# A hybrid decoder block on one core: block sums of the tokens with four operations a round, and a third raw tile for the memory's weights

## The chip, the cores and the metric

The kernel runs on one core of a Trainium2 chip. The metric is the device time of one execution in microseconds; the times of before are those of three runs. TensorE (PE, with its weight loads PEld), VectorE (DVE), ScalarE (ACT), GpSimd (POOL) and the DMA queue of SyncE (SP) each work through their own list of instructions in order, and wait for each other by semaphores.

## The reference

One decoder layer over 1024 tokens of width 1024, all in float32. Three gated branches read the same normalised tokens; what is computed, cut to what matters here:

```python
h = rmsnorm(x, g_mix_norm[l])
proj = jnp.einsum('bsd,de->bse', h, w_in[l])
sb_q, sb_k, sb_v, fx_q, fx_k, fx_v, f_logit, m_q, gate_logit = split_columns(proj, SPLITS)
o_sb = stick_breaking_attention(...)      # 8 heads of 64
o_fox = forgetting_attention(...)         # 8 heads of 64
mh = rmsnorm(mem, g_mem_norm[l])          # 256 memory tokens
mkv = jnp.einsum('bmd,de->bme', mh, w_mem_kv[l])
mk, mv = split_columns(mkv, (D_MEM, D_MEM))
mq, mk = rmsnorm(...), rmsnorm(...)
o_mem = memory_attention(mq, mk, mv)      # 4 heads of 128
merged = gates[:, :, 0] * br_sb + gates[:, :, 1] * br_fox + gates[:, :, 2] * br_mem
x = x + jnp.einsum('bsd,de->bse', merged, w_out[l])
u = jax.nn.relu(jnp.einsum('bsd,df->bsf', rmsnorm(x, g_mlp_norm[l]), w_ff_up[l]))
x = x + jnp.einsum('bsf,fd->bsd', u * u, w_ff_down[l])
```

## The kernel before

**Products.** Each float32 operand is split into a high part, rounded by ScalarE, and a low part, which VectorE makes by a subtraction. A product is three matmuls: high by high, high by low, low by high. A weight therefore goes through a fetch into a raw tile, ScalarE (`split`, line 1149) and VectorE (line 1150) before TensorE can use it. In the profile `ha`, `hb`, `hc` are the three high tiles of weights, `la`, `lb`, `lc` their low tiles, and `ra`, `rb` the two raw tiles that weights are fetched into.

**The order of the work.** Most of the kernel is written as coroutines. A small planner in the kernel's own Python runs them with guessed costs, one list of ready operations for each engine, and emits the instructions in the order in which it would have begun them. Tiles are handed out by `Places`, queues of free tiles: who asks first gets the tile that was freed first. The order on each engine, and which tile serves whom, follow from that plan and are fixed in the program.

**The stretch of the change.** It begins after the prologue has normalised and turned the tokens, at about 55 us, and ends where the large projections begin, at 113.8 us. Dense tasks run one after the other on TensorE (`dense`, matmul line 1239): the values of the forgetting heads with the forget logits (`fx1`), one gate task (`dense_gate(9)`, weight in `hb`/`lb`), and then four tasks of the memory, `kv_tasks`, here called kv0 to kv3. A memory task (`dense_kv`) has two weights of 512 rows by 256 columns (512 KB each), and runs four quarters of 12 matmuls: first weight, second weight for one half of the memory tokens, then both again for the other half. The three pairs of weight tiles go round: kv0 uses `ha` and `hc`, kv1 `hb` and `ha`, kv2 `hc` and `hb`, kv3 `ha` and `hc`, and the first projection unit `hb` again. From 113.8 us on the projection units (`unit_products`, line 1551) take over.

`loader` picks the tasks in turn, asks for their raw tiles (`RAW`, two of them) and issues the fetches on SP; `weight` waits for a fetch, splits it and gives the raw tile back. `ahead` holds the raw tiles that were asked for before the splits.

**The sums of tokens.** Beside that, `sums_T` makes sums of blocks of the normalised tokens, operands of the projection units, in four rounds, one for each 128 rows of the model width. `hTh`, `hTl` are the high and low parts of the tokens (`h`, `g` in the profile); `b11` is the round's piece of the first block. `second_half` fetches the two pieces of the other token half (`t1`, `t2`, tiles `sn`) from memory. A round makes `t1 - b11`, `t2 - t1` and `t2 - b11`, where `b11` is subtracted in its two parts, and splits the three results into the operand tiles `T_of` (`both`, through `split`: a ScalarE half `h<-sn` and a VectorE half `h<-sn,h` each). After the memory tasks four further rounds (lines 655 to 657) follow.

The pool `t` with these operands, and the pool `r` with the raw blocks of `w_in`, are closed in `second_part`, when the last of them has been read; the tiles of the attention take their place.

Of the kernel before, what the change touches and what calls it, by code (L numbers as in the profile page):

```python
# [31 lines left out]
WS = 4 * 264  # L32
# [6 lines left out]
def f32(ap):  # L39
    return ap.bitcast(F32)  # L40
# [3 lines left out]
def tile_hybrid_block(  # L44
# [23 lines left out]
    nc = tc.nc  # L68
# [229 lines left out]
    def dve_time(*cols):  # L298
        return sum(0.08 + 0.00105 * m for m in cols)
# [50 lines left out]
    holder = {}  # L350
# [10 lines left out]
        return Places([pool.t(tag, [P, shape], dt) for _ in range(n)])  # L361

    PP, SC, TR, PV = (banks(tag) for tag in ("pp", "sc", "tr", "pv"))
    ES, OO, EL, RR, HT, PH, PL, OB, VV, BK, LATER, NONE, RQ = (Places([]) for _ in range(13))
    SN, RS, S1 = tiles(E, "sn", 10, 512), tiles(R, "raw", 4, 1024), R.t("s1", [P, 4, 256])
    XT, BC = tiles(N, "xt", 8, D), tiles(N, "bc", 4, P)
    made_w = {tag: [] for tag in SLOTS}
# [208 lines left out]
    def prologue():  # L576

        keys = [[("x", s)] for s in range(ST)] + [[("m", 0), ("m", 1)]]
        xs = [("x", s) for s in range(2, PLAIN)] + [(k_, s) for s in range(PLAIN, ST) for k_ in ("x", "xt")]
        spawn(fetch_tokens([("x", 0), ("g", "x"), ("x", 1), ("w", 0), ("w", 1), *xs[:1], ("g", "xt"), *xs[1:], ("g", "mt"),  # L580
                            *[(k_, s) for s in range(2) for k_ in ("m", "mt")]]))
        spawn(warm(half_made[2, 1]), 100.0)
        evs = [spawn(norm(ks_, 4.0 * i - 8.0, half_made[AFTER[i]] if i in AFTER else None), 4.0 * i - 8.0)
               for i, ks_ in enumerate(keys)]
        for ev in evs:
            yield ev
        spawn(small_loads())
# [27 lines left out]
    def sums_T():  # L615
# [2 lines left out]
        coming = spawn(second_half(0))  # L618
        for k in range(4):
            b11 = tuple(t[:, k, 0:512] for t in (hTh, hTl))  # L620
            yield coming
            t1, t2 = fetched_h[k]
            if k < 3:
                coming = spawn(second_half(k + 1))
            w_ = yield Get(SN)

            def first():
                nc.vector.tensor_tensor(t1, t1, f32(b11[0]), ALU.subtract)
                nc.vector.tensor_tensor(t1, t1, f32(b11[1]), ALU.subtract)

            def second():
                nc.vector.tensor_tensor(t2, t2, t1, ALU.subtract)
# [503 lines left out]
        machine.fire(pair.v_made)  # L1136


    queue, state = deque(), {"loading": True}

    class Task:

# [13 lines left out]
            m = src.shape[1]  # L1156
            queue_.dma_start(view[:, :, off:off + m], src.rearrange("(k p) n -> p k n", p=P))

    def weight(pair, load, raw):
        _, kk, n = load  # L1160
        if raw is None:
            raw = yield Get(RAW)
            if kv_over.fired:
                yield spawn(transfer(lambda: fetch(raw, load, nc.gpsimd), P * kk * n * 4, 0.8, queue_="POOL"), -30.0)
            else:
                yield from transfer(lambda: fetch(raw, load), P * kk * n * 4)
        else:
            raw, ev = raw
            yield ev
        yield from split(pair[0][:, :kk * n], pair[1][:, :kk * n], raw[:, :kk * n])  # L1170
        RAW.put(raw)

    def loader(tasks):
        while tasks:
# [4 lines left out]
            tasks.remove(t)  # L1179
            queue.append(t)  # L1180
            machine.fire(t.chosen)
            ahead = []
            for load in t.loads:
                if fetched:
                    ahead.append((fetched.popleft(), True))
                elif len(ahead) < 2 if not kv_over.fired else t is branches[0] and not ahead:
                    raw = (yield Get(RAW)), Event()
                    spawn(landed(lambda raw=raw, load=load: fetch(raw[0], load), P * load[1] * load[2] * 4, raw[1]))
                    ahead.append((raw, False))
            for load in t.loads:  # L1190
                raw, first = ahead.pop(0) if ahead else (None, False)
# [3 lines left out]
                t.w.append((spawn(weight(pair, load, raw), -6.0 if first or t is h_tasks[0] else 1.0), pair, views))  # L1195
            while queue:
                yield Sleep(0.2)
        state["loading"] = False
# [514 lines left out]
    def second_part():  # L1713
# [1142 lines left out]
```

## Time and profile before

| | us |
|---|---|
| three runs | 1656.91, 1657.71, 1659.15 |
| median | 1657.71 |
| the profiled execution | 1657.59 |
| its span on the core | 1655.8 |
| TensorE matmul busy in the span | 1646.7 |
| VectorE busy | 1293.4 |
| ScalarE busy | 849.5 |

The span runs from the first to the last instruction; 1.8 us of the profiled execution's time lie around it. The granted TensorE clock is at full speed over the span (0.999 on average). A row of the timeline gives start, length, engine, source line, operation, output and inputs; in brackets behind it, the idle time before it and what ended it. A row of the waits gives who waited for whom, the microseconds in total, the number of waits and the longest. Matmul ends are modelled and overlap the next matmul's start.

### The profile page before, as it was taken

How to read it: one execution, taken by the hardware profiler on the slowest of the kernel's cores; microseconds unless marked ns; L12 is line 12 of the kernel's file. 1: busy time of each engine (PE TensorE's matmuls, PEld its weight loads, DVE VectorE, ACT ScalarE, POOL GpSimd, SP SyncE). 2: the span in 40 equal slices, each digit the busy share in tenths (PEclk: the TensorE clock that was granted, in tenths of full speed). 3: DMA queues.
4: the chain of work that ended last, by engine and by line, in shares of the span. 5: the costliest groups of instructions: out<-in, count | busy, mean ns of one | idle time of the engine just before them, and what ended most of it. 6: DMA issues, size and time to landing. Idle time of an engine off the chain costs nothing.

```text
span 1655.8 us, 25062 instructions
## 1 busy us (share of the span) xinstructions
PE 1646.7 (99%) x9082; PEld 1429.4 (86%) x9082; DVE 1293.4 (78%) x2123; ACT 849.5 (51%) x1476; POOL 254.8 (15%) x440
## 2 busy tenths in 40 slices
PE   9999999999999999999999999999999999999999
PEld 8988899998888988888888888888888888888887
DVE  7798789955549888868877798987777777788875
ACT  6355555535458898977772465533233345233331
POOL 0000000000153232245400011021221120000000
PEclk9999999999999999999999999999999999999999
DMA  9846655568474455477866762154444475564532
GB/s 331 254 142 200 213 165 187 169 183 252 146 245 137 150 155 169 138 222 223 219 167 216 256 231 98 52 178 146 156 156 153 146 285 198 193 215 158 203 127 76
DMA packets 153629, 302.68 MB, mean 183 GB/s; under 512 B 18081, under 2 KB 58593, under 8 KB 153122
## 3 DMA queue, kind: packets, MB, share of 16 engines
q1 hardware_dynamic: 121970, 201.45, 36.2%
q0 software_dynamic: 31536, 99.64, 19.6%
q8 instruction: 71, 1.16, 0.3%
q14 instruction: 52, 0.43, 0.1%
HBM read 201.89 MB, written 99.13 MB: 182 GB/s over the span
## 4 chain that ended last, share of the span: by engine, by line
PE 94%; DVE 3%; DMA 2%; ACT 1%; issue 0%; SPq 0%
PE pp L1551 11%; PE pp L1239 9%; PE pp L2101 9%; PE pp L2791 8%; PE sc L1551 7%; PE sc L1239 6%; PE sc L2101 5%; PE tr L2791 4%; PE sc L2791 4%; PE tr L1012 4%; PE pv L1551 3%; PE pv L2791 3%; PE sc L1029 2%; PE tr L2101 2%; PE pp L1029 2%; PE pp L2346 2%
## 5 line engine op out<-in xcount | busy, mean ns | idle before, releaser
L1019 DVE TENSOR_TENSOR ptl<-tr,pth 128x512 fp32r<-128x512 f32 (+1 forms) x160 | 99.1, 628 | 25.5 <-ACT pth L1017 24.5
L2101 PE MATMUL pp<-h,oh 128*128 128x512 f32 x384 | 118.3, 389 | 0.0
L1017 ACT ACTIVATE pth<-tr 128x512 fp32r<-128x512 f32 (+1 forms) x160 | 87.5, 557 | 33.5 <-PE sc L1029 13.9
L2189 ACT ACTIVATE cu<-pp 128x512 f32<-128x512 f32 x48 | 28.7, 598 | 137.3 <-PE pp L2101 137.3
L2101 PEld LDWEIGHTS pp<-h,oh 128*128 128x128 f32 x384 | 72.0, 188 | 15.0 <-ACT oh L2532 0.2
L1468 POOL DMA_DIRECT2D raw<-w_in x32 | 24.2, 757 | 393.3 <-DVE lc L1150 205.2
L2101 PE MATMUL pp<-h,ol 128*128 128x512 f32 x192 | 74.9, 390 | 0.5 <-DVE ol L2037 0.5
L938 DVE TENSOR_TENSOR_SCAN e<-r,e 128x384 f32<-128x384 f32 (+3 forms) x64 | 66.3, 1044 | 6.8 <-ACT e L923 6.4
L2791 PE MATMUL pp<-h,h 128*128 128x512 f32 x288 | 66.6, 389 | 0.0
L2791 PE MATMUL pp<-sop,sop 128*128 128x512 f32 x288 | 66.6, 389 | 0.0
L2791 PEld LDWEIGHTS pp<-h,h 128*128 128x128 f32 x288 | 54.1, 188 | 11.2
L2791 PEld LDWEIGHTS pp<-sop,sop 128*128 128x128 f32 x288 | 54.1, 188 | 11.2
L1012 PE MATMUL tr<-ident,e 128*128 128x128 f32 x416 | 62.5, 273 | 0.0
L1012 PEld LDWEIGHTS tr<-ident,e 128*128 128x128 f32 x416 | 50.5, 140 | 9.9
L2118 POOL DMA_DIRECT2D s_scr<-cu x48 | 26.1, 544 | 189.3 <-DVE cu L2108 179.8
L1029 PE MATMUL sc<-pth,v 128*128 128x256 f32 (+1 forms) x174 | 48.0, 298 | 0.0
L2037 DVE TENSOR_TENSOR cu<-cu,sc 128x512 f32<-128x512 f32 x33 | 22.5, 682 | 32.5 <-ACT cu L2189 32.5
L1099 POOL DMA_DIRECT2D h<-sbk_scr x64 | 33.3, 527 | 94.1 <-PE pv L156 29.5
L2706 ACT ACTIVATE h<-t 128x2048 fp32r<-128x2048 f32 (+1 forms) x9 | 15.4, 1724 | 59.5 <-DVE t L2037 55.4
L2037 DVE TENSOR_TENSOR x<-x,pp 128x512 f32<-128x512 f32 x39 | 26.6, 683 | 22.8 <-PE pp L2791 22.8
L2101 PEld LDWEIGHTS pp<-h,ol 128*128 128x128 f32 x192 | 36.0, 188 | 8.7 <-DVE ol L2037 1.2
L2118 POOL DMA_DIRECT2D s_scr<-s x60 | 32.5, 542 | 71.0 <-DVE s L2037 64.4
(797 smaller groups left out, 5546.7 us busy)
## 6 DMA issues: line engine op xcount, KB each, us to landing
ur<-s_scr SPq DMA_DIRECT2D x26, 1024.0 KB
raw<-w_in POOLq DMA_DIRECT2D x32, 512.0 KB, 5.2
raw<-w_up SPq DMA_DIRECT2D x60, 256.0 KB
s_scr<-s POOLq DMA_DIRECT2D x60, 256.0 KB, 2.5
g<-w_down SPq DMA_DIRECT2D x14, 1024.0 KB
s_scr<-cu POOLq DMA_DIRECT2D x48, 256.0 KB, 2.3
h<-sbk_scr POOLq DMA_DIRECT2D x64, 128.0 KB, 3.1
o<-gate_scr SPq DMA_DIRECT2D x32, 256.0 KB
```

The source lines that it names most:

```text
L938: nc.vector.tensor_tensor_scan(out=back, data0=rho[:, :u][:, ::-1], data1=back, initial=0.0 if last else beta[:, c + u:c + u + 1], op0=ALU ...
L1012: nc.tensor.transpose(tr[:, jj * 256 + a * P:jj * 256 + (a + 1) * P], es[a][:, j * P:(j + 1) * P], ident)
L1017: yield Op("ACT", act_time(512 - lo_c), lambda: nc.scalar.activation(ph[:, lo_c:], tr[:, lo_c:], AF.Copy))
L1019: yield Op("DVE", dve_time(512 - lo_c), lambda: nc.vector.tensor_tensor(pl[:, lo_c:], tr[:, lo_c:], f32(ph[:, lo_c:]), ALU.subtract))
L1029: nc.tensor.matmul(pv[0][:, c_:256], pair.v[:, j, b, :], p_[:, jj * 256 + c_:(jj + 1) * 256], start=(k == 0 and n_ == 0 and i == 0), stop= ...
L1099: nc.gpsimd.dma_start(f32(t[k][rows_, :]), src)
L1239: nc.tensor.matmul(ps, a_, b_, start=(first and i == 0), stop=(last and i == n - 1))
L1551: nc.tensor.matmul(out_, a_, b_, start=(first and n == 0 and j == 0), stop=(last and n == 3 and j == len(todo) - 1), skip_group_check=True)
L2037: nc.vector.tensor_tensor(out_, a_, b_, op)
L2101: nc.tensor.matmul(ps, w[a_][:, k * P:(k + 1) * P], h[b_][k], start=(first and k == 0 and i == 0), stop=(last and k == 3 and i == 2), skip ...
L2118: nc.gpsimd.dma_start(s_scr[r0:r0 + P, :], t)
L2791: nc.tensor.matmul(ps, a_[:, c, qs], b_[:, c, :], start=(kind in ("P1", "P2", "P7") and c == 0 and i == 0), stop=(kind in ("P2", "P4", "P3 ...
```

## The change

In `sums_T` a round first adds the two parts of `b11` into a tile `w_` and then subtracts that one tile twice: four operations of 128x512 on VectorE in place of five. The addition stands ahead of the wait for the fetched pieces, so `w_` is taken before it.

A pool `t3` with one raw tile more is opened after the prologue and handed out through a place of its own, `EXTRA`. When `loader` has spawned the weights of a task and the next task is one of the memory's, it takes that tile, if it is free, and fetches the next task's first weight into it; the pieces kept in `early_raws` become the next task's `ahead`. `weight` gives each raw tile back to the place that it came from. In the program that results, the third tile (`raw_908`) holds kv1's first weight and then kv2's first weight; kv0 and kv3 go through `ra` and `rb` as before.

```diff
+        holder["T3"] = Pool("t3", raw=1)
+        EXTRA.put(holder["T3"].t("raw", [P, WS]))
...
         for k in range(4):
             b11 = tuple(t[:, k, 0:512] for t in (hTh, hTl))
+            w_ = yield Get(SN)
+            yield Op("DVE", dve_time(512), lambda: nc.vector.tensor_tensor(w_, f32(b11[0]), f32(b11[1]), ALU.add))
             yield coming
             t1, t2 = fetched_h[k]
             if k < 3:
                 coming = spawn(second_half(k + 1))
-            w_ = yield Get(SN)
 
             def first():
-                nc.vector.tensor_tensor(t1, t1, f32(b11[0]), ALU.subtract)
-                nc.vector.tensor_tensor(t1, t1, f32(b11[1]), ALU.subtract)
+                nc.vector.tensor_tensor(t1, t1, w_, ALU.subtract)
...
             def third():
-                nc.vector.tensor_tensor(w_, t2, f32(b11[0]), ALU.subtract)
-                nc.vector.tensor_tensor(w_, w_, f32(b11[1]), ALU.subtract)
+                nc.vector.tensor_tensor(w_, t2, w_, ALU.subtract)
...
-    def weight(pair, load, raw):
+    def weight(pair, load, raw, place):
...
-        RAW.put(raw)
+        place.put(raw)
...
-            ahead = []
+            ahead, early_raws[:] = early_raws[:], []
+            for load in t.loads[len(ahead):]:
+                if fetched:
+                    ahead.append((fetched.popleft(), True, RAW))
+                elif len(ahead) < 2 if not kv_over.fired else t is branches[0] and not ahead:
+                    place = RAW
+                    raw = (yield Get(place)), Event()
+                    spawn(landed(lambda raw=raw, load=load: fetch(raw[0], load), P * load[1] * load[2] * 4, raw[1]))
+                    ahead.append((raw, False, place))
...
+            if tasks and tasks[0] in kv_tasks and EXTRA.free:
+                load, raw = tasks[0].loads[0], ((yield Get(EXTRA)), Event())
+                spawn(landed(lambda raw=raw, load=load: fetch(raw[0], load), P * load[1] * load[2] * 4, raw[1]))
+                early_raws.append((raw, False, EXTRA))
...
+        holder["T3"].close()
         holder["T"].close()
```

The order of the instructions changes on SP, ScalarE, VectorE and TensorE between the gate task and the first projection unit; elsewhere only the numbers of tiles differ. Below, before stands first and after second; line 1157 of before is line 1158 of after, 1149 and 1150 are 1150 and 1151, 609 and 610 are 611 and 612, 1338 is 1344, 1753 is 1760, 1757 is 1764.

On SP, the fetches of the memory's weights (`w_kv`), with the last store of values, the last pair of fetched pieces (`h_scr`, round 3) and the two gate stores between them, before:

```order
L1157 DMA ra_174<-w_kv 128x4x256
L1157 DMA rb_176<-w_kv 128x4x256
L1338 DMA v_fx_95<-sn_148 128x512
L609 DMA sn_154<-h_scr 128x512
L610 DMA sn_147<-h_scr 128x512
L1757 DMA gate_scr<-sn_150 128x512
L1157 DMA ra_174<-w_kv 128x4x256
L1157 DMA rb_176<-w_kv 128x4x256
L1757 DMA gate_scr<-sn_155 128x512
```

and after:

```order
L1158 DMA ra_174<-w_kv 128x4x256
L1158 DMA rb_176<-w_kv 128x4x256
L1158 DMA raw_908<-w_kv 128x4x256
L1344 DMA v_fx_95<-sn_149 128x512
L611 DMA sn_148<-h_scr 128x512
L612 DMA sn_147<-h_scr 128x512
L1764 DMA gate_scr<-sn_151 128x512
L1158 DMA ra_174<-w_kv 128x4x256
L1764 DMA gate_scr<-sn_146 128x512
L1158 DMA raw_908<-w_kv 128x4x256
L1158 DMA rb_176<-w_kv 128x4x256
```

kv1's first weight moved ahead of a store, the pair of pieces and a gate store, and kv2's first weight follows in the same tile.

On ScalarE, from the high part of kv0's first weight (`ha`) on, with the rounding of the sums (`h<-sn`) and the evictions of the gate task (`sn<-pp`), before:

```order
L1149 ACTIVATE ha_173<-ra_174 128x1024
L1149 ACTIVATE hc_177<-rb_176 128x1024
L1753 ACTIVATE sn_150<-pp_138 128x512
L1149 ACTIVATE h_907<-sn_152 128x512
L1149 ACTIVATE h_905<-sn_151 128x512
L1149 ACTIVATE h_909<-sn_149 128x512
L1753 ACTIVATE sn_155<-pp_139 128x512
L1149 ACTIVATE h_907<-sn_147 128x512
L1149 ACTIVATE h_905<-sn_154 128x512
L1149 ACTIVATE hb_179<-ra_174 128x1024
L1149 ACTIVATE h_909<-sn_146 128x512
L1149 ACTIVATE ha_173<-rb_176 128x1024
```

and after:

```order
L1150 ACTIVATE ha_173<-ra_174 128x1024
L1150 ACTIVATE h_911<-sn_154 128x512
L1150 ACTIVATE h_913<-sn_150 128x512
L1150 ACTIVATE h_909<-sn_152 128x512
L1150 ACTIVATE hc_177<-rb_176 128x1024
L1760 ACTIVATE sn_151<-pp_138 128x512
L1760 ACTIVATE sn_146<-pp_139 128x512
L1150 ACTIVATE h_911<-sn_147 128x512
L1150 ACTIVATE hb_179<-raw_908 128x1024
L1150 ACTIVATE h_913<-sn_155 128x512
L1150 ACTIVATE h_909<-sn_148 128x512
L1150 ACTIVATE ha_173<-ra_174 128x1024
```

The three halves of round 2 moved ahead of `hc`, and kv1's `hb` moved ahead of two halves of round 3, where it stood behind two.

On VectorE, round 3 of the sums with kv1's two low parts, before:

```order
L628 TENSOR_TENSOR sn_154<-sn_154,h_125 128x512
L629 TENSOR_TENSOR sn_154<-sn_154,h_129 128x512
L632 TENSOR_TENSOR sn_147<-sn_147,sn_154 128x512
L635 TENSOR_TENSOR sn_146<-sn_147,h_125 128x512
L636 TENSOR_TENSOR sn_146<-sn_146,h_129 128x512
L1150 TENSOR_TENSOR h_908<-sn_147,h_907 128x512
L1150 TENSOR_TENSOR h_906<-sn_154,h_905 128x512
L1150 TENSOR_TENSOR lb_180<-ra_174,hb_179 128x1024
L1150 TENSOR_TENSOR h_910<-sn_146,h_909 128x512
L1150 TENSOR_TENSOR la_175<-rb_176,ha_173 128x1024
```

and after (line 624 is the new addition, 631 and 637 the two subtractions of `w_`):

```order
L1151 TENSOR_TENSOR lc_178<-rb_176,hc_177 128x1024
L624 TENSOR_TENSOR sn_155<-h_125,h_129 128x512
L631 TENSOR_TENSOR sn_148<-sn_148,sn_155 128x512
L634 TENSOR_TENSOR sn_147<-sn_147,sn_148 128x512
L637 TENSOR_TENSOR sn_155<-sn_147,sn_155 128x512
L1151 TENSOR_TENSOR h_912<-sn_147,h_911 128x512
L1151 TENSOR_TENSOR lb_180<-raw_908,hb_179 128x1024
L1151 TENSOR_TENSOR h_914<-sn_155,h_913 128x512
L1151 TENSOR_TENSOR h_910<-sn_148,h_909 128x512
L1151 TENSOR_TENSOR la_175<-ra_174,ha_173 128x1024
```

`lb` stands one operation of the round and one half sooner; the rest of round 2, which before stood between kv0's `lc` and round 3, now stands ahead of `lc`.

On TensorE the sequence of matmuls is the same but for two small groups: two matmuls on the identity that stood between kv0 and kv1 now stand between kv1 and kv2, and four transposes for the memory's keys (line 827) that stood between kv2 and kv3 now stand behind kv3's first quarter.

More of the change, by code (lines that the diff above doesn't have):

```diff
@@ L363, in tile_hybrid_block @@
     PP, SC, TR, PV = (banks(tag) for tag in ("pp", "sc", "tr", "pv"))
-    ES, OO, EL, RR, HT, PH, PL, OB, VV, BK, LATER, NONE, RQ = (Places([]) for _ in range(13))
+    ES, OO, EL, RR, HT, PH, PL, OB, VV, BK, LATER, NONE, RQ, EXTRA = (Places([]) for _ in range(14))
     SN, RS, S1 = tiles(E, "sn", 10, 512), tiles(R, "raw", 4, 1024), R.t("s1", [P, 4, 256])
@@ L634, in third @@
             def third():
-                nc.vector.tensor_tensor(w_, t2, f32(b11[0]), ALU.subtract)
-                nc.vector.tensor_tensor(w_, w_, f32(b11[1]), ALU.subtract)
-            yield Op("DVE", dve_time(512, 512), first)
+                nc.vector.tensor_tensor(w_, t2, w_, ALU.subtract)
+            yield Op("DVE", dve_time(512), first)
             yield Op("DVE", dve_time(512), second)
             two = [spawn(both("P6", k, t2)), spawn(both("P5", k, t1), 2.0)]
-            yield Op("DVE", dve_time(512, 512), third)
+            yield Op("DVE", dve_time(512), third)
             two.append(spawn(both("P7", k, w_), 1.0))
@@ L1136, in load_v @@
         machine.fire(pair.v_made)
-    queue, state = deque(), {"loading": True}
+    queue, early_raws, state = deque(), [], {"loading": True}
     class Task:
@@ L1181, in loader @@
             machine.fire(t.chosen)
-            ahead = []
-            for load in t.loads:
[L1184 to L1191, printed above, removed]
+            ahead, early_raws[:] = early_raws[:], []
[7 more added lines that the diff above has]
+                    ahead.append((raw, False, place))
+            for load in t.loads:
+                raw, first, place = ahead.pop(0) if ahead else (None, False, RAW)
                 pair = yield Get(WP)
@@ L1194, in loader @@
                 views = tuple(w_[:, :kk * n].rearrange("p (k n) -> p k n", n=n) for w_ in pair)
-                t.w.append((spawn(weight(pair, load, raw), -6.0 if first or t is h_tasks[0] else 1.0), pair, views))
+                t.w.append((spawn(weight(pair, load, raw, place), -6.0 if first or t is h_tasks[0] else 1.0), pair, views))
+            if tasks and tasks[0] in kv_tasks and EXTRA.free:
+                load, raw = tasks[0].loads[0], ((yield Get(EXTRA)), Event())
+                spawn(landed(lambda raw=raw, load=load: fetch(raw[0], load), P * load[1] * load[2] * 4, raw[1]))
+                early_raws.append((raw, False, EXTRA))
             while queue:
```

## The prediction

> **What bounds the kernel now.** I read the page first, then the windows around the change, then the waits of the tensor engine over the whole span.
>
> ```profile
> PE 1646.7 (99%) x9082; PEld 1429.4 (86%) x9082; DVE 1293.4 (78%) x2123; ACT 849.5 (51%) x1476; POOL 254.8 (15%) x440
> PE 94%; DVE 3%; DMA 2%; ACT 1%; issue 0%; SPq 0%
> 60.00:80.00 20.00, 20.00 (x153) 19.33 (x152) 14.31 (x31) 5.99 (x13) 0.00 (x0) 1.00 0.70 206
> 80.00:100.00 20.00, 18.82 (x127) 17.17 (x126) 17.28 (x28) 10.79 (x16) 0.00 (x0) 1.00 0.55 177
> 100.00:120.00 20.00, 19.59 (x139) 18.19 (x138) 18.86 (x27) 11.10 (x16) 0.00 (x0) 1.00 0.47 159
> 120.00:140.00 20.00, 20.00 (x90) 16.58 (x89) 16.02 (x22) 9.09 (x14) 3.19 (x4) 1.00 0.45 134
> PE pp L1239 <- DVE lb L1150: 1.5, 2, 1.1
> ```
>
> TensorE is the bound (94% of the chain that ended last). A saved VectorE operation is therefore worth nothing by itself; it pays only where TensorE waits. The window rows (length, then busy time of PE, PEld, DVE, ACT, POOL, granted clock, DMA share, GB/s) show TensorE full from 60 to 80 and from 120 on. It has holes from 80 to 120, and the largest PE wait of the whole kernel lies there: the memory's weights (`lb`), twice (1.5 us in total, 1.1 the longer).
>
> How large the holes are is read from start times, because a matmul's shown end overlaps the next one's start:
>
> ```profile
> 86.94 0.39 PE L1239 MATMUL pp<-g,lb 128*128 128x512 f32 x1
> 88.60 0.28 PE L1239 MATMUL pp<-hc,mt 128*128 128x256 f32 x1
> 93.06 0.36 PE L1239 MATMUL pp<-hb,mt 128*128 128x256 f32 x1
> 94.56 0.39 PE L1239 MATMUL pp<-lb,mt 128*128 128x256 f32 x1 [1.14 <-DVE lb L1150]
> 95.98 0.28 PE L1239 MATMUL pp<-ha,mt 128*128 128x256 f32 x1
> 96.30 0.39 PE L1239 MATMUL pp<-la,mt 128*128 128x256 f32 x1
> 97.72 0.28 PE L1239 MATMUL pp<-hb,mt 128*128 128x256 f32 x1
> 97.84 0.28 PE L1239 MATMUL pp<-lb,mt 128*128 128x256 f32 x1
> 102.04 0.60 PE L827 MATMUL tr<-ident,sn 128*128 128x128 f32 x4
> 102.39 0.36 PE L1239 MATMUL pp<-hb,mt 128*128 128x256 f32 x1
> 103.16 0.39 PE L1239 MATMUL pp<-lb,mt 128*128 128x256 f32 x1 [0.41 <-DVE lb L1150]
> 113.84 0.63 PE L1551 MATMUL pp<-h,hb 128*128 128x512 f32 x2
> ```
>
> Undisturbed, the start-to-start step is 0.12 us (97.72 to 97.84), so a quarter of a memory task (12 matmuls on one weight) is 1.44 us, and kv0, whose second quarter begins at 88.60, ends at 92.9. Four transposes take 0.35 (102.04 to 102.39). The three disturbed steps cost 94.56-93.06-0.12 = 1.38 (kv1's first weight), 96.30-95.98-0.12 = 0.20 (kv1's second), 103.16-102.39-0.12 = 0.65 (kv2's second). Sum 2.23 us; that is about what this change can win at the most, since the next task's matmuls (113.84) follow without a hole.
>
> A page of the Trainium skill changes this term: "Perfetto Trace Analysis", section Identifying the Most-Contended Engine, says that matmul busy is a poor measure of tensor headroom, because the pipelined instructions mislead. By PE busy the holes are 1.18 + 0.41 = 1.59 us, and the forecast would be 0.6 us later; the start times give 2.23, so the trace agrees with the page here.
>
> **The change part by part.** Why kv1's weights are late stands on three queues:
>
> ```profile
> 72.06 0.38 SPq L609 DMA_DIRECT2D sn<-h_scr  x1
> 73.30 0.32 SPq L610 DMA_DIRECT2D sn<-h_scr  x1
> 74.82 0.43 SPq L1157 DMA_DIRECT2D ra<-w_kv  x1
> 75.31 0.55 SPq L1157 DMA_DIRECT2D rb<-w_kv  x1
> 84.48 0.38 SPq L1157 DMA_DIRECT2D ra<-w_kv  x1
> 94.54 0.37 SPq L1157 DMA_DIRECT2D ra<-w_kv  x1
> 103.14 0.37 SPq L1157 DMA_DIRECT2D rb<-w_kv  x1
> 78.45 0.42 DVE L1332 TENSOR_TENSOR sn<-pp,sn 128x256 fp32r<-128x256 f32 x1
> 80.06 0.68 DVE L628 TENSOR_TENSOR sn<-sn,h 128x512 f32<-128x512 f32 x1
> 80.78 0.69 DVE L629 TENSOR_TENSOR sn<-sn,h 128x512 f32<-128x512 f32 x1
> 82.20 1.23 DVE L1150 TENSOR_TENSOR la<-ra,ha 128x1024 fp32r<-128x1024 f32 x1 [0.73 <-ACT ha L1149]
> 84.72 0.68 DVE L632 TENSOR_TENSOR sn<-sn,sn 128x512 f32<-128x512 f32 x1
> 93.29 1.22 DVE L1150 TENSOR_TENSOR lb<-ra,hb 128x1024 fp32r<-128x1024 f32 x1
> 108.26 1.22 DVE L1150 TENSOR_TENSOR lc<-rb,hc 128x1024 fp32r<-128x1024 f32 x1 [0.15 <-ACT hc L1149]
> 81.11 1.06 ACT L1149 ACTIVATE ha<-ra 128x1024 fp32r<-128x1024 f32 x1 [2.51 <-DMA ra<-w_kv]
> 82.48 1.06 ACT L1149 ACTIVATE hc<-rb 128x1024 fp32r<-128x1024 f32 x1 [0.32 <-DMA rb<-w_kv]
> 90.75 1.15 ACT L1149 ACTIVATE h<-sn 128x512 fp32r<-128x512 f32 x2 [2.72 <-DVE sn L632]
> 91.81 1.04 ACT L1149 ACTIVATE hb<-ra 128x1024 fp32r<-128x1024 f32 x1
> 98.18 1.06 ACT L1149 ACTIVATE hc<-ra 128x1024 fp32r<-128x1024 f32 x1 [1.01 <-DMA ra<-w_kv]
> 107.17 1.06 ACT L1149 ACTIVATE hc<-rb 128x1024 fp32r<-128x1024 f32 x1 [2.15 <-DMA rb<-w_kv]
> L629 DVE TENSOR_TENSOR sn<-sn,h 128x512 f32<-128x512 f32 x4 | 2.8, 692 | 0.1
> ```
>
> kv1's first weight is fetched into `ra` only after kv0's split of `ra` (82.20 + 1.23 = 83.4; issued 84.48). Its high part (91.81) did not wait for it: ScalarE stood before two halves of the sums of round 3, which waited 2.72 us for VectorE. VectorE did the rest of round 2 and all of round 3 between 84.72 and 93.29.
>
> (1) *One operation fewer a round.* Four rounds lose one 128x512 operation of 0.69 us (L629's row): 2.8 us of VectorE. Of each remaining four, the first no longer needs the fetched half, so it runs ahead of it. Rounds 0 and 1 follow the evictions of TensorE; the two operations saved in rounds 2 and 3 (1.4 us) stand ahead of `lb`. That is the hole which the third tile also fills, so I count it once, below; beyond that the saving is worth nothing, as VectorE is not the bound.
>
> (2) *The third raw tile.* kv1's first weight is issued right behind `rb`, 75.31 + 0.55 = 75.9 instead of 84.48. `ra` and `rb` of the same size landed 1.37 us apart (81.11, 82.48), so I put it at 82.48 + 1.37 = 83.9. It then waits for ScalarE and for `hb`, which the gate task reads up to 86.94. Behind it on SP stand a store of values, the last pair of fetched halves and gate stores; they come at most 0.55 us (issue) plus 1.37 us (transfer) later. Of these only round 3's pair has a reader soon, at 87 by (3), some three microseconds after the third tile's 83.9; nothing on TensorE waits.
>
> (3) *The moved splits, worked out by hand.* Steps: a 1024-wide split is 1.06 on ScalarE and 1.15 to 1.23 on VectorE; a 512-wide VectorE step is 0.60, or 0.72 where it needs the one before (80.06 to 80.78); a 512-wide half on ScalarE is 0.58 (90.75's row). Round 2 starts at 78.6 (by my walk the last value eviction, 78.45 before, now starts at 77.5) and is over at 80.7, before `la` at 82.20. Then three halves and `lc` (to 86.4), round 3 (to 89.1), `hb` at 89.0, `lb` 90.1 to 91.3; TensorE wants it at 93.0: 1.7 us to spare. `ha` must wait for the end of kv0's third quarter (88.60 + 23 x 0.12 = 91.4), so `la` is ready at 93.7 against 94.5: 0.8 to spare. The 1.38 and the 0.20 go.
>
> kv2's first weight goes into the third tile again, behind `lb`: issued 91.3, landing 3.6 us later (94.54 to 98.18), 95.0. Its second needs `hb`, free at 97.3, so `lb` is ready at 99.5; TensorE, now at kv2 from 98.8, wants it a quarter and four transposes later, at 100.6. The 0.65 goes as well.
>
> (4) *What is late next.* kv3's second weight goes into `rb` after that `lb` (99.5), lands 4.0 us later (103.14 to 107.17) at 103.6, is rounded by 104.7, and its low part stands behind a 1.2 us sum on VectorE: ready at 107.0, wanted at 106.8 to 106.9 (kv3 from 104.9, a quarter and four transposes on). I take 0.1 us of new wait; its ends are 0 and 0.65, the size of the same wait before.
>
> (5) *The SP queue ahead.* The new issue costs SP 0.55 us (75.31's row) at 75.9, where SP next waits for the eviction that ends at 78.9 (78.45 + 0.42): hidden, and worth 0.55 us if that cover went.
>
> Sum: 1.38 + 0.20 + 0.65 - 0.1 = 2.1 us. After 120 us TensorE is full, so it starts each later piece 2.1 us sooner, and its feeders, released by TensorE or by each other, move with it; if they kept their old times instead, the gain would shrink to 0. The profiled execution took 1657.59 us (span 1655.8), 0.12 below the median of the three runs, 1657.71. 1657.59 - 2.1 gives **1655.5 us**, 0.13% less. A difference of 0.2% (3.3 us) is about what a measurement of this kernel can tell from no change, so this counts as within it.
>
> **The rivals.**
> - *No gain: the feeders do not move.* VectorE is busy 18.86 of 20 us from 100 to 120; if its queue there were already the limit, TensorE would win 2.1 us at 113 and wait it back. For it: that busy time. Against it: kv3's `lc` itself, which starts that stretch, ends 2.5 us sooner in (4) than 109.5 before (108.26 + 1.22). Time 1657.6.
> - *Transfers share instead of queueing.* If the third fetch takes bandwidth from `ra` and `rb` at once, both land up to 1.37 us later; the chain of (3) then has kv1's `la` at 95.0 instead of 93.7, wanted at 94.5: 0.5 us back, time 1656.0. Against it: `ra` and `rb` landed one after the other although issued 0.5 us apart. The Trainium skill, "DMA: Bandwidth & Descriptors", section Queues, rings and completion order, has each DMA engine take descriptors in ring order; by that rule this rival falls away, and the landing times agree.
> - *Slower: kv0's second weight behind the sums on ScalarE.* In the new order `hc` for kv0 stands behind three halves of round 2, the last of which need that round's fetched pair (issued 72.06 and 73.30). Before, it came ahead of them. If the pair lands at T, `hc` starts at about T + 0.72 + 0.72 + 0.69 + 1.2 = T + 3.3, and `lc` is ready at T + 5.7; kv0 wants it at 88.6. It decides from T = 82.9, and every microsecond beyond is lost on TensorE; to be 0.2% slower it must also eat the gain: T = 88.3. Against it: the pair's first half was read at 80.06 without a wait, and both were issued ahead of `ra`, which landed at 81.11. At T = 88.3 the time would be 1661.
> - *More than the holes.* Over 0.2% faster needs 3.3 us, more than all of 2.23; it would have to take holes that the waits do not show, say another 1.2 us: 1654.2.
> - *The change does not do what it says.* The third tile serves only two of the four tasks (kv1 and kv2); if its fetch brought nothing, (1) alone would bring `lb` forward by up to 1.4 us and fill the first hole: 1656.2.
>
> **How the numbers follow.** Forecast 0.62; shared transfers 0.08; feeders do not move 0.08; the third tile does not help 0.06; more than the holes 0.11; slower 0.05. The cases at 1655.5, 1656.0, 1657.6 and 1656.2 lie within 0.2%: 0.84. So faster 0.11, same 0.84, slower 0.05. The three runs of before spread by 2.2 us (1656.91 to 1659.15), and a median moves by about half of that. The range runs from the forecast less that half and the 0.1 of (4), 1654.3, rounded down to 1654.0 for part of the case with more than the holes, up to the case of no gain with the same half, 1658.2 rounded.
>
> **What would show each step.** A third-tile fetch at 75.9 on SP, with `hb` starting near 89.0 and no wait by TensorE on `lb` (step 2, 3); four VectorE operations fewer and busy time lower by 2.8 us (1); the unit products starting at 111.7 instead of 113.84 (sum); a short wait for `lc` near 107 (4); and the same 2.1 us still there at the end. Wrong would be: the unit products earlier but the span unchanged (first rival), a TensorE wait for `lc` near 88.6 (third), or `hb` still starting near 91.8 (last).

## The result, and the profile after

The changed kernel takes 1655.8 us (median of 18 runs; from 1654.75 up), the kernel before on the same chip 1658.95 us (median of 18 runs, 1656.58 to 1660.69). The ratio is 0.9982, 95% interval 0.9976 to 0.9988: by it 3.0 us less (2.0 to 4.0), just inside the 0.2% that was to count as no change. One run of the changed kernel (5864.84 us) and the profiled run of tile_only below (2337.79 us, with TensorE's clock granted at 0.654 throughout) were slow runs: they count in the medians given here but not in the ratios, and without them the medians are 1655.64 and 1657.37 us. The profiled execution took 1656.32 us (span 1654.6, before 1655.8).

The page's busy times and its chain, then the windows, of the kernel after:

```profile
PE 1646.5 (100%) x9082; PEld 1428.8 (86%) x9082; DVE 1289.9 (78%) x2119; ACT 849.7 (51%) x1476; POOL 255.9 (15%) x440
PE 95%; DVE 2%; DMA 1%; ACT 1%; issue 0%; SPq 0%
```

```profile
80.00:100.00 20.00, 20.00 (x140) 18.71 (x139) 16.64 (x25) 12.67 (x19) 0.00 (x0) 1.00 0.64 215
100.00:120.00 20.00, 19.99 (x135) 18.36 (x134) 18.62 (x27) 9.97 (x15) 0.00 (x0) 1.00 0.38 132
```

TensorE's busy time is the same and VectorE has four operations and 3.5 us less. The two windows that had holes (18.82 and 19.59 us busy) are full. The rows that answer to the prediction's, in the timeline of after (start, length, engine, line, operation, output and inputs):

```profile
76.11 0.68 SPq L1158 DMA_DIRECT2D raw<-w_kv  x1
91.45 0.38 SPq L1158 DMA_DIRECT2D raw<-w_kv  x1
81.24 1.06 ACT L1150 ACTIVATE ha<-ra 128x1024 fp32r<-128x1024 f32 x1 [4.04 <-DMA ra<-w_kv]
89.13 1.04 ACT L1150 ACTIVATE hb<-raw 128x1024 fp32r<-128x1024 f32 x1
90.20 1.23 DVE L1151 TENSOR_TENSOR lb<-raw,hb 128x1024 fp32r<-128x1024 f32 x1 [0.26 <-ACT hb L1150]
93.00 1.23 DVE L1151 TENSOR_TENSOR la<-ra,ha 128x1024 fp32r<-128x1024 f32 x1 [0.37 <-ACT ha L1150]
98.76 1.23 DVE L1151 TENSOR_TENSOR lb<-rb,hb 128x1024 fp32r<-128x1024 f32 x1 [0.52 <-ACT hb L1150]
105.03 1.22 DVE L1487 TENSOR_TENSOR s<-raw,raw 128x1024 f32<-128x1024 f32 x1
106.16 1.22 DVE L1151 TENSOR_TENSOR lc<-rb,hc 128x1024 fp32r<-128x1024 f32 x1
93.09 0.28 PE L1245 MATMUL pp<-hb,mt 128*128 128x256 f32 x1
93.21 0.28 PE L1245 MATMUL pp<-lb,mt 128*128 128x256 f32 x1
107.06 0.36 PE L1245 MATMUL pp<-hc,mt 128*128 128x256 f32 x1
107.43 0.39 PE L1245 MATMUL pp<-lc,mt 128*128 128x256 f32 x1
111.73 0.63 PE L1557 MATMUL pp<-h,hb 128*128 128x512 f32 x2
```

kv1's low part is over at 91.43, TensorE steps from `hb` to `lb` at 93.21 in 0.12 us, and the unit products start at 111.73 (113.84 before). One new wait stands at 107.43: 0.37 from `hc` to `lc`, 0.25 more than an undisturbed step of 0.12; in before the same step took 0.20, so 0.17 of it is new.

To see where time is kept and lost, each matmul of a trace is set beside the same matmul of before's trace; the difference of the two start times is called the shift. "Stretch" is how much the shift changes between before's 92 and 113.84 us; the last columns are the times. Every kernel stands in this table; the experiments follow below. tile_only has no trace that can be set beside before's.

| kernel | stretch | shift at 113.84 | at 700 | at 900 | at the end | median us | ratio to before (95%) |
|---|---|---|---|---|---|---|---|
| after | -2.27 | -2.10 | -2.06 | -1.42 | -1.27 | 1655.80 | 0.9982 (0.9976 to 0.9988) |
| after_again | -2.28 | -2.12 | -2.10 | -2.34 | -2.38 | 1655.44 | 0.9986 (0.9977 to 0.9995) |
| before_again | +0.63 | +0.89 | +0.98 | +5.59 | +5.65 | 1658.29 | 1.0001 (0.9992 to 1.0009) |
| sums_only | -2.16 | -2.19 | -2.16 | -1.21 | -1.25 | 1656.33 | 0.9987 (0.9978 to 0.9996) |
| tile_only | - | - | - | - | - | 1657.48 | 0.9995 (0.9986 to 1.0004) |
| tile_again | -1.29 | -1.07 | -1.09 | -1.31 | -1.35 | 1656.74 | 0.9991 (0.9982 to 1.0000) |
| six_ops | +1.43 | +1.33 | +1.34 | +1.33 | +1.87 | 1658.90 | 1.0006 (0.9997 to 1.0015) |
| plus_half | +0.11 | +0.10 | +0.12 | +1.15 | +1.12 | 1659.06 | 1.0001 (0.9992 to 1.0011) |
| plus_one | +0.22 | +0.16 | +0.11 | +0.54 | +1.25 | 1658.98 | 1.0007 (0.9998 to 1.0017) |
| plus_two | +3.01 | +3.15 | +3.14 | +3.14 | +3.15 | 1660.58 | 1.0018 (1.0008 to 1.0027) |
| lc_ahead | -2.56 | -2.26 | -1.09 | -0.76 | -0.74 | 1657.49 | 0.9995 (0.9987 to 1.0004) |
| later_sum | -2.26 | -1.80 | -1.83 | -1.92 | -1.41 | 1656.60 | 0.9991 (0.9982 to 1.0000) |

The shift of after is made in the stretch, stays for six hundred microseconds, and shrinks by 0.7 us near 732 us in this one execution.

### The profile page after: what moved, and what is told of

Its sections match the earlier page's. It is cut to its first block, busy times and chain, and to the rows that moved or that the text cites. A ratio compares the mean times of both kernels' runs of the same rounds, so it can differ in the third digit from the quotient of the medians.

```text
span 1654.6 us, 25061 instructions
## 1 busy us (share of the span) xinstructions
PE 1646.5 (100%) x9082; PEld 1428.8 (86%) x9082; DVE 1289.9 (78%) x2119; ACT 849.7 (51%) x1476; POOL 255.9 (15%) x440
## 3 DMA queue, kind: packets, MB, share of 16 engines
q8 instruction: 71, 1.16, 0.3%
## 4 chain that ended last, share of the span: by engine, by line
PE 95%; DVE 2%; DMA 1%; ACT 1%; issue 0%; SPq 0%
PE pp L1557 11%; PE pp L1245 11%; PE pp L2108 9%; PE pp L2798 8%; PE sc L1557 7%; PE sc L1245 6%; PE sc L2108 5%; PE sc L2798 4%; PE tr L2798 4%; PE tr L1013 4%; PE pv L1557 3%; PE pv L2798 3%; PE sc L1030 2%; PE tr L2108 2%; PE pp L2353 2%; PE pp L1030 2%
## 5 line engine op out<-in xcount | busy, mean ns | idle before, releaser
L1151 DVE TENSOR_TENSOR lb<-raw,hb 128x1024 fp32r<-128x1024 f32 x21 | 25.7, 1222 | 23.0 <-ACT hb L1150 23.0
```

## The experiments

**sums_only and tile_only: one half of the change each.** sums_only has the four-operation rounds and no third tile; tile_only the third tile and rounds of five operations.

```diff
 sums_only, against the kernel before
+            w_ = yield Get(SN)
+            yield Op("DVE", dve_time(512), lambda: nc.vector.tensor_tensor(w_, f32(b11[0]), f32(b11[1]), ALU.add))
             yield coming
...
-                nc.vector.tensor_tensor(t1, t1, f32(b11[0]), ALU.subtract)
-                nc.vector.tensor_tensor(t1, t1, f32(b11[1]), ALU.subtract)
+                nc.vector.tensor_tensor(t1, t1, w_, ALU.subtract)
...
```

```diff
 tile_only, against the kernel before
+        holder["T3"] = Pool("t3", raw=1)
+        EXTRA.put(holder["T3"].t("raw", [P, WS]))
...
+            if tasks and tasks[0] in kv_tasks and EXTRA.free:
+                load, raw = tasks[0].loads[0], ((yield Get(EXTRA)), Event())
...
```

> Only the sums' part of the change: four operations a round, no third raw tile. Theory A (the holes were VectorE's and ScalarE's queue, not the fetch): kv1's hb still goes through ra, fetched near 85.7 us and landed near 90; hb near 90.3, lb ready near 92.5, wanted at 93.0, la near 93.7, wanted at 94.5. No wait of TensorE on lb, unit products from 111.7 to 112.1 us, about 2.0 us less than before. Rival B (the fetch was the cause, so the third tile does it): hb still near 91.8, lb after 94, a wait of 1 us or more on lb, gain under 0.7 us.

> Only the third raw tile and the early fetch; the rounds of sums keep five operations. Theory A: kv1's first hole goes (hb near 88.0, lb ready near 91.2), but its second weight now stands behind more of round 3: la ready near 95.7, wanted at 94.5, a wait of about 1.2 us; the wait at kv2 goes. Gain about 1.0 us, unit products near 112.9 us. Rival B (the third tile does it): no wait on lb or la beyond 0.2 us, gain about 2.1 us.

In the traces the sums alone bring nearly everything: the stretch shrinks by 2.16 us against 2.27 with both parts, and TensorE waits for `lb` and `la` no more. The times can't tell the two kernels apart: the ratios are 0.9987 and 0.9986 (after_again, from the same set of runs), the medians 1656.33 and 1655.44. The timeline of sums_only:

```profile
80.04 0.69 DVE L635 TENSOR_TENSOR sn<-sn,sn 128x512 f32<-128x512 f32 x1
82.03 1.23 DVE L1149 TENSOR_TENSOR la<-ra,ha 128x1024 fp32r<-128x1024 f32 x1 [1.29 <-ACT ha L1148]
85.44 0.38 SPq L1156 DMA_DIRECT2D ra<-w_kv  x1
80.93 1.06 ACT L1148 ACTIVATE ha<-ra 128x1024 fp32r<-128x1024 f32 x1 [3.94 <-DMA ra<-w_kv]
90.06 1.04 ACT L1148 ACTIVATE hb<-ra 128x1024 fp32r<-128x1024 f32 x1
91.14 1.22 DVE L1149 TENSOR_TENSOR lb<-ra,hb 128x1024 fp32r<-128x1024 f32 x1 [0.17 <-ACT hb L1148]
99.52 1.23 DVE L1149 TENSOR_TENSOR lb<-rb,hb 128x1024 fp32r<-128x1024 f32 x1 [0.73 <-ACT hb L1148]
93.23 0.28 PE L1238 MATMUL pp<-lb,mt 128*128 128x256 f32 x1
100.86 0.33 PE L1238 MATMUL pp<-lb,mt 128*128 128x256 f32 x1
```

kv1's first weight is fetched into `ra` at 85.44, later than the 84.48 of before, and still `lb` is over at 92.36, 0.9 us before TensorE reads it. The late fetch was not what made the weight late.

Only part of this is the operation saved in round 3. In before, three operations of round 2 stood behind `la` (from 84.72 on); here round 2 is over ahead of `la` (its last operation starts at 80.04), in time in which VectorE waits for `ha` anyway (1.29 us). Between `la` and `lb` there are four operations of 128x512 instead of eight, and one half more. The hole at kv2 goes as well: its second weight can be fetched into `rb` as soon as kv1's `la` is over, which is at 94.01 instead of 96.25, so its `lb` starts 2.4 us sooner (99.52 instead of 101.89), while TensorE comes there only 1.7 us sooner.

The times of tile_only (0.4 us less than before by medians, which can't be told from none) agree with a part of the gain only.

**tile_again: the third tile alone, once more for its trace.**

> The third raw tile alone, with the sums at five operations a round. Theory A (the hole is VectorE's queue ahead of the weight's low part; the tile helps only as far as the split of kv1's first weight is let in between the sums): that split starts near 88.0 on ScalarE and the wait for lb at kv1 goes, but the rest of round 3 then stands ahead of kv1's second weight, so TensorE waits for la there, about 1.2 us; unit products start at 112.7 to 113.2 (113.84 before, 111.73 with both parts), time 1656.4 to 1657.2. Theory B (the late fetch made the hole): all three holes go and unit products start at 111.7, as with both parts.

Theory A holds: `hb` starts at 88.20, the unit products at 112.77, and the wait has moved to kv1's second weight, where it is 0.8 us instead of 1.2. TensorE's waits and the timeline of tile_again:

```profile
PE pp L1246 <- DVE la L1152: 0.8, 1, 0.8
```

```profile
88.20 1.05 ACT L1151 ACTIVATE hb<-raw 128x1024 fp32r<-128x1024 f32 x1
90.20 1.22 DVE L1152 TENSOR_TENSOR lb<-raw,hb 128x1024 fp32r<-128x1024 f32 x1
93.39 1.29 DVE L1152 TENSOR_TENSOR h<-sn,h 128x512 fp32r<-128x512 f32 x2
94.60 1.22 DVE L1152 TENSOR_TENSOR la<-ra,ha 128x1024 fp32r<-128x1024 f32 x1
95.87 0.39 PE L1246 MATMUL pp<-la,mt 128*128 128x256 f32 x1 [0.79 <-DVE la L1152]
```

The tile lets `lb` in before the end of round 3; what is left of the round then stands ahead of `la`. Alone it wins 1.29 us of the 2.27.

**six_ops: one VectorE operation more a round.** The opposite of the first half of the change, without the tile.

```diff
             def first():
+                nc.vector.tensor_tensor(w_, f32(b11[0]), f32(b11[1]), ALU.add)
                 nc.vector.tensor_tensor(t1, t1, f32(b11[0]), ALU.subtract)
...
-            yield Op("DVE", dve_time(512, 512), first)
+            yield Op("DVE", dve_time(512, 512, 512), first)
```

> The kernel before with a sixth 128x512 VectorE operation in each round of the sums (an extra sum into a tile that is overwritten later), no third tile. Theory A (VectorE's queue ahead of the weight): two more operations of 0.69 us stand in rounds 2 and 3, one of them partly inside the 0.7 us in which VectorE waited for ha, so kv1's lb comes 0.1 to 0.8 us later than in the kernel before, la follows it with no gap, and the unit products start at 114.0 to 115.0 instead of 113.84: time 1657.9 to 1659. Theory B (the fetch of ra, which cannot be issued before kv0's split is over): lb stays where it was and unit products start at 113.8 within 0.15.

The timeline of six_ops:

```profile
88.33 1.05 ACT L1150 ACTIVATE hb<-ra 128x1024 fp32r<-128x1024 f32 x1
89.18 0.68 DVE L628 TENSOR_TENSOR sn<-h,h 128x512 f32<-128x512 f32 x1
93.90 1.22 DVE L1151 TENSOR_TENSOR lb<-ra,hb 128x1024 fp32r<-128x1024 f32 x1
95.17 0.38 PE L1240 MATMUL pp<-lb,mt 128*128 128x256 f32 x1 [1.85 <-DVE lb L1151]
```

This tells the queue from the fetch: the high part is ready at 89.4, 3.5 us sooner than before (the planner put its split ahead of the halves), and the low part starts only at 93.90, behind seven operations of round 3. The Trainium skill, "Perfetto Trace Analysis", section Tensor Engine Instruction (MATMUL, LD_WEIGHTS), calls ScalarE's and VectorE's queues strict FIFO; these rows agree: 4.5 us of a ready operation waiting its turn. `lb` came 0.6 us later than before (93.90 and 93.29), as expected by theory A; the unit products came at 115.17, 0.17 past its upper end, for a reason of its own (last section).

**plus_half, plus_one, plus_two: a measured dose.** The instructions and their order are those of before, with an addition put in at the head of the last round: 128x256, 128x512, and two of 128x512. The planner is not told of them, so nothing else moves. The edit of plus_one:

```diff
             def first():
+                if k == 3:
+                    nc.vector.tensor_tensor(w_, f32(b11[0]), f32(b11[1]), ALU.add)
                 nc.vector.tensor_tensor(t1, t1, f32(b11[0]), ALU.subtract)
```

> The kernel before, its order of instructions unchanged, with one addition of 128x256 on VectorE (about 0.4 us) put into the last round of the sums, ahead of kv1's lb; its result is overwritten. Theory A (what VectorE gets ahead of lb comes out on TensorE one for one): the wait for lb at kv1 grows from 1.14 to about 1.5 us and the unit products start 0.4 us later than in the kernel before, at 114.2. Theory B (a long wait also lowers the granted clock of TensorE for some microseconds after it, as it stood at 0.57 from 96 to 100 us behind a wait of 1.85 us in the kernel with six operations, against 1.00 behind 1.14 us): at 1.5 us either, 114.2 with the clock at 1.00, or up to 115.3 with it near 0.6. Theory C (lb is bound by its fetch): 113.84, nothing later.

> As the kernel with the 128x256 addition, but 128x512 (0.6 to 0.7 us). Theory A: wait 1.75 to 1.85 us, unit products at 114.5. Theory B: clock near 0.57 for about 3.7 us after the wait, which costs 1.1 to 1.6 us more, unit products at 115.6 to 116.1. Theory C: 113.84.

> As the kernel with the 128x256 addition, but two of 128x512 (1.3 us). Theory A: wait 2.4 to 2.5 us, unit products at 115.1 to 115.2. Theory B: clock near 0.57 for about 3.7 us after the wait, unit products at 116.2 to 116.8. Theory C: 113.84.

The sizes missed: the stretch grew by 0.11, 0.22 and 3.01 us, where theory A had 0.4, 0.7 and 1.3, one for one. The unit products started at 113.94, 114.00 and 116.99 us, and TensorE's waits were 0.17 + 1.27, 1.27 and 1.99 + 1.28 us (for `hb` and `lb`, or for `lb` alone). The rows of ScalarE and VectorE say why the waits came out so. In plus_two, the first use of kv0's `ra` after its landing, then kv1's `lb`:

```profile
82.31 1.06 ACT L1152 ACTIVATE ha<-ra 128x1024 fp32r<-128x1024 f32 x1 [3.57 <-DMA ra<-w_kv]
95.83 1.22 DVE L1153 TENSOR_TENSOR lb<-ra,hb 128x1024 fp32r<-128x1024 f32 x1
```

The landing of kv0's first weight varies from execution to execution, and what VectorE does from `la` to `lb` is counted from it. The distance between the two starts, over all traces of the stretch:

| kernel | ra issued | ha<-ra starts | lb starts | distance |
|---|---|---|---|---|
| before | 74.82 | 81.11 | 93.29 | 12.18 |
| before_again | 75.08 | 81.93 | 94.12 | 12.19 |
| plus_half | 74.81 | 81.32 | 93.85 | 12.53 |
| plus_one | 74.76 | 80.64 | 93.44 | 12.80 |
| plus_two | 74.97 | 82.31 | 95.83 | 13.52 |
| six_ops | 75.35 | 80.38 | 93.90 | 13.52 |
| sums_only | 74.82 | 80.93 | 91.14 | 10.21 |
| lc_ahead | 75.16 | 81.05 | 91.26 | 10.21 |
| tile_again | 75.05 | 81.33 | 90.20 | 8.87 |
| after | 75.03 | 81.24 | 90.20 | 8.96 |
| after_again | 75.01 | 81.67 | 90.63 | 8.96 |
| later_sum | 75.32 | 81.39 | 90.36 | 8.97 |

Programs that are equal up to `lb` agree to 0.01 us, and the doses come out as 0.35, 0.62 and 1.34 us for additions of 0.33, 0.61 and 1.33 (start to start). (six_ops is a different case: its `la`, at 83.05, waited for VectorE and not for `ha`.) So as far as `lb` theory A holds, and theory C falls: from the landing of `ra` to `lb` there is no slack on VectorE in the kernel before, and each operation in it counts in full.

As far as the unit products theory A does not hold. What reaches them also depends on when `ra` lands, on the clock (last section), and on the hole at kv2, which can swallow a delay. In plus_half the shift stays at +0.56 from kv1's `lb` up to that hole and is 0.00 behind it:

```profile
102.95 0.36 PE L1241 MATMUL pp<-hb,mt 128*128 128x256 f32 x1
103.16 0.38 PE L1241 MATMUL pp<-lb,mt 128*128 128x256 f32 x1
```

The step is 0.21 us, where before it was 0.77, and `lb` is read at the same 103.16. In this execution `rb`, the raw tile of that weight, was used 3.95 us after its issue (96.84 to 100.79), in before 4.51 us (96.28 to 100.79). The same place takes 0.1 us from plus_one and 0.67 us from plus_two and six_ops.

This also gives an estimate of what the third tile is for. `lb` must be over, 1.2 us after its start, by about 93.2. With the four-operation sums alone that holds while `ha<-ra` starts before 93.2 - 1.2 - 10.2 = 81.8; with the tile as well, before 83.0. Of the twelve starts above, two lie past 81.8 (81.93, 82.31) and none past 83.0. By this estimate the tile is worth 0.1 to 0.5 us in such executions and nothing in the others; no run here shows sums_only with so late a landing.

**after_again and before_again: the same kernels once more.** Do the 0.7 us that after lost at 732 us belong to the change?

> The changed kernel once more, for a second profile and times beside the parts. Theory A: 2.1 us sooner at the first unit product, and the 0.7 us that the first profile lost near 732 us (a fetch of the heads' outputs that landed later against its issue) is a matter of the single execution: it is not there again, or is of another size. Rival C: it is there again with the same 0.7 us, a fixed loss of the moved schedule. Ratio 0.998 to 0.999.

> The kernel before against itself: how far two sets of its runs lie apart, and where two profiles of it differ. Both theories: ratio within 0.9995 to 1.0005; the three holes at 94.6, 96.3 and 103.2 us again with 1.4, 0.2 and 0.65 us.

They don't: after_again keeps its 2.1 us there and ends at -2.38. What differs is one fetch of a head's output, issued at the same time and landed at another; SP's issue and the ScalarE split that reads it, in after, then in after_again:

```profile
725.16 0.33 SPq L1786 DMA_DIRECT2D r<-o_scr  x1
728.89 0.63 ACT L1150 ACTIVATE h<-r 128x512 fp32r<-128x512 f32 x1 [1.92 <-DMA r<-o_scr]
```

```profile
725.12 0.33 SPq L1786 DMA_DIRECT2D r<-o_scr  x1
727.73 0.63 ACT L1150 ACTIVATE h<-r 128x512 fp32r<-128x512 f32 x1 [0.66 <-DMA r<-o_scr]
```

3.73 us from issue to use in the one, 2.61 in the other, with evictions that TensorE needs behind the split on ScalarE. before_again has the same kind of place at 829 us, on VectorE, and lost 3.9 us there (its timeline and windows):

```profile
820.71 2.06 SPq L1782 DMA_DIRECT2D r<-low_scr  x1
831.37 1.23 DVE L1784 TENSOR_TENSOR r<-r,r 128x1024 f32<-128x1024 f32 x1 [2.57 <-DMA r<-low_scr]
833.25 0.33 PE L964 MATMUL pp<-h,h 128*128 128x128 f32 x1 [2.07 <-DVE st L969]
```

```profile
830.00:835.00 5.00, 2.93 (x13) 2.07 (x12) 3.63 (x9) 0.46 (x2) 0.00 (x0) 0.87 0.91 280
835.00:840.00 5.00, 5.00 (x29) 4.55 (x29) 2.03 (x10) 3.98 (x9) 0.00 (x0) 0.79 0.64 143
```

The sum `r<-r,r` waited 2.57 us for its fetch with TensorE's evictions behind it. sums_only lost 1.1 us between 780 and 900 us; its sum waited 0.83 us for the same fetch. Such places and the landing of `ra` make most of the difference in the two pairs of traces of one program (after and after_again, before and before_again); that they do so in the other runs is not shown.

before_again has the three holes again, with 1.54, 0.20 and 0.76 us where 1.4, 0.2 and 0.65 were expected, and 0.4 us more just ahead of them, at `hb`; its `ra` was used 0.8 us later. So the stretch of one and the same program can differ by 0.6 us between executions.

**lc_ahead: the new wait of the prediction's (4), taken away.** sums_only, with the unit's block sums planned 1 us later, so that `lc` stands ahead of the first of them.

```diff
         yield kv_taken
+        yield Sleep(1.0)
         for u in PROJ:
```

> The four-operation sums without the third tile, and the sums of the unit's blocks planned 1 us later, so that the low part of kv3's second weight (lc) stands ahead of the first of them on VectorE. Theory A (that 1.2 us sum is what made lc late near 107): the wait goes, unit products start at 111.4 instead of 111.64 with the four-operation sums alone, and TensorE stays full after that. Theory B (the block sums, now later, make a unit weight late): the 0.25 us won is lost in a new wait between 112 and 120. Time in both cases within 0.3 us of the four-operation sums alone (1656.3), which the runs cannot tell apart; the trace decides.

The timeline of lc_ahead, then two rows of sums_only:

```profile
105.29 1.23 DVE L1149 TENSOR_TENSOR lc<-rb,hc 128x1024 fp32r<-128x1024 f32 x1
118.43 1.22 DVE L1481 TENSOR_TENSOR raw<-raw,raw 128x1024 f32<-128x1024 f32 x1
122.70 1.22 DVE L1149 TENSOR_TENSOR lc<-raw,hc 128x1024 fp32r<-128x1024 f32 x1
123.97 0.50 PE L1551 MATMUL pp<-h,lc 128*128 128x512 f32 x1 [0.87 <-DVE lc L1149]
```

```profile
106.07 1.22 DVE L1149 TENSOR_TENSOR lc<-rb,hc 128x1024 fp32r<-128x1024 f32 x1
119.32 1.22 DVE L1149 TENSOR_TENSOR lc<-raw,hc 128x1024 fp32r<-128x1024 f32 x1
```

Theory A is right about the wait: `lc` starts 0.8 us sooner (105.29 and 106.07), the stretch is the shortest of all (-2.56), and the unit products start at 111.58 (111.4 expected). Theory B is right about the rest, though the new wait comes at 124 us and not before 120: with the block sums between (118.43), the unit's third weight is split 3.4 us later than in sums_only, and 1.16 us are lost. VectorE has little room there (18.62 of 20 us busy from 100 to 120 in the windows of after), and here the operation put ahead made another late. The time was expected within 0.3 us of sums_only's 1656.33 and came out at 1657.49, about what the new wait costs.

**later_sum: the sum at 829 us put behind TensorE's evictions.** The changed kernel, with

```diff
-            yield Sleep(1.0 if k == ks[3] else 2.0)
+            yield Sleep(1.0 if k == ks[3] else 4.0)
             yield Op("DVE", dve_time(S), lambda: nc.vector.tensor_tensor(raw, raw, t, ALU.add))
```

> The changed kernel with the sum of the two parts of the heads' outputs (r + r, after two fetches) planned 2 us later, so that it stands behind the evictions which TensorE waits for near 829 us instead of ahead of them. Theory A (single executions lose 0.3 to 2 us there since this sum waits for its fetch with the evictions behind it): the shift against the kernel before stays at -2.1 us or better past 829 us, and the median falls by 0.2 to 0.6 us against the changed kernel, to about 1655.1. Theory B (the order also moves products and evictions further on): new waits eat it, 1655.4 to 1657.

Not confirmed. The shift at 900 us is -1.92, so this execution lost nothing at 829, but the time did not fall: 1656.60, ratio 0.9991. The planner also reordered products between 790 and 870 us. One trace doesn't tell whether that cost the difference or the landings elsewhere did. No version here shows as faster than the changed kernel.

## Why the prediction was right, and where it was not

- **The size of the holes** (1.38 + 0.20 + 0.65 = 2.23 us from start times) was right in the main: at the same three steps the shift falls by 1.38, 0.20 and 0.57, and by another 0.10 or 0.11 at the step behind each, which had been slow too (0.22 to 0.23 us) and which the prediction left out. The new wait for `lc` takes 0.17 back. The stretch is 2.27 us shorter, where 2.1 was forecast. The unit products start at 111.73, predicted 111.7; that this is so close is partly luck, since the prologue of this execution alone was 0.17 us later. By TensorE's busy time the sum would have been 1.59.
- **(1), the saved operations, was mis-sized, and it is the main error.** The prediction gave the saving nothing of its own beyond the hole that the third tile "also fills", 1.4 us of two operations, and the rival "(1) alone" one hole, 1656.2. In sums_only it fills all three: `lb` starts 12.18 - 10.21 = 1.97 us sooner after `ha`, because three operations of round 2 move ahead of `la` as well, and the splits behind it move up. That sums_only's median, 1656.33, lies at the rival's time says nothing for the rival: its trace has 2.16 us in the stretch, and lost 1.1 us later. The text's own reading, that ScalarE and VectorE stood behind the sums, already held this; I drew the third tile from the late fetch (issued at 84.48) though `hb` had not waited for it. VectorE's busy time fell by 3.5 us instead of 2.8, but two profiles of before differ by 1.7 us in it.
- **(2), the third tile, was right in its times and not in its worth.** Issued at 76.11 (75.9), `hb` at 89.13 (89.0), again at 91.45 (91.3). Beside the shorter sums it adds 0.1 us in these traces; by the times its worth stays open (medians 0.9 us apart, ratios 0.0001).
- **(3), the walk by hand, was right within 0.5 us:** `lb` over at 91.43 (91.3), kv1's `la` at 94.23 (93.7), kv2's second `lb` at 99.99 (99.5), and the prologue of this execution alone was 0.2 us later. A long walk along in-order queues from measured durations held here.
- **(4), the new wait for `lc`,** came where it was put, at 107, and took 0.25 us instead of 0.1 (0.17 more than the same step before), inside its ends of 0 and 0.65; lc_ahead shows that the 1.2 us sum ahead of it was the cause.
- **(5)** held: the issue of 0.68 us at 76.11 made nobody wait.
- **The rivals.** "Feeders do not move" showed up as a matter of single executions: 0.7 us lost near 732 us, by a late landing, not by VectorE's load. "Transfers share": `ra` landed in time for 81.24, 81.67 and 81.39 with the third fetch behind it and for 80.38 to 82.31 without, so it takes nothing that can be seen. `hc` for kv0 behind the sums cost nothing. Nothing beyond the holes was won in the stretch.
- **Time.** 1655.5 was predicted, 1655.8 and 1655.44 measured, and here too luck had a part. The forecast took 2.1 us off the profiled execution of before (1657.59), which lies 1.4 us under the median of its 18 runs, 1658.95. By medians the difference is 2.5 to 3.2 us; the low start and the low gain cancel. Between the two profiled executions it is only 1.27, as that of after lost 0.7 us at 732. What the medians have beyond the 2.27 us of the stretch is not shown. One candidate is the landing of `ra`: a late one cost before_again 0.63 us in the stretch, while the changed kernel kept its 2.26 to 2.28 in all three executions with `ha` at 81.24 to 81.67.

## What to carry to other kernels

A wait that names a weight is not yet a wait for its fetch: look at what stands ahead of the weight's last operation on its in-order engine, and ask whether the operations before it waited for the transfer at all. A buffer and a shorter queue can fill the same hole, so their gains don't add (2.16 and 1.29 us alone, 2.27 together); build each alone before crediting both. A delay at one wait can vanish in a later one, so follow the shift through all of them. To size a dose below the spread between runs, measure it in the trace from the event that starts the chain (here the landing of `ra`), not from the start of the span or in the total time.

## What the runs showed of the hardware

A long wait of TensorE cost more than itself here. Behind 1.14 us (before) and behind 0.17 + 1.27 us (plus_half) the granted clock stayed at 1.00. Behind 1.85 us it fell; the windows of six_ops, and of plus_two after waits of 1.99 and 1.28 us:

```profile
96.00:98.00 2.00, 2.00 (x13) 2.00 (x12) 2.00 (x4) 0.00 (x0) 0.00 (x0) 0.58 0.81 270
98.00:100.00 2.00, 2.00 (x13) 2.00 (x12) 1.24 (x7) 1.35 (x2) 0.00 (x0) 0.57 0.81 237
```

```profile
96.00:98.00 2.00, 0.90 (x4) 0.90 (x5) 2.00 (x3) 1.82 (x3) 0.00 (x0) 0.71 0.00 0
98.00:100.00 2.00, 2.00 (x11) 2.00 (x11) 1.77 (x5) 0.30 (x1) 0.00 (x0) 0.50 0.75 265
```

These windows are averages. In finer ones six_ops has 1.00 up to 96.3, 0.50 from 96.4 to 99.7 and 1.00 from 99.8 us on: half the clock for about 3.4 us, beginning 1.2 us after TensorE had resumed at 95.17. It is as long in plus_two (0.50 until 100.2) and before_again (0.50 from 833.8 to 837.0). Matmuls then stand 0.21 us apart instead of 0.12. That cost six_ops another 1.2 us (its shift goes from +0.61 to +1.80 in the quarters after the wait), and plus_two 1.1 (+2.54 to +3.61); before_again lost about 1.6 us behind the 2.07 us at 833. This is theory B of the dose: it came at all three waits of 1.85 us and more, and behind none of the shorter ones. These are the 1.14 to 1.27 us for `lb` (plus_one's own wait came out at 1.27), and waits in the prologue, the longest of them 1.68 us (six_ops, at 7.45 us; the clock reads 1.00 from 7 to 12 us). No trace at full clock has a wait between 1.68 and 1.85 us, so where it begins, and whether it comes each time, is open. The Trainium skill, "TensorE: Matmul & The Clock Gate", section What's actually happening, has the clock halve after an idle window of about 3.4 us that runs free of the kernel; the traces agree with the half clock (0.50), but the waits here were shorter than that window, so the measured 1.85 us decides.

The other thing is the landing time of a fetch: 5.0 to 7.3 us from issue to use for the 512 KB of `ra` in twelve executions, and 2.6 to 3.7 us for the head's output at 725 us.
